# The norm ahead of the last feed-forward block: four of eight squares summed on TensorE, the sums and the spread one product sooner, the last output projection in order

## The chip, the cores and the metric

The kernel runs on one core of one Trainium2 chip. The metric is the time of one execution in microseconds on the device, lower is better. The engines are TensorE (PE in the profile, with its weight loads as PEld), VectorE (DVE), ScalarE (ACT), GpSimd (POOL) and SyncE (SP, which issues most transfers).

## The reference

One step of a streaming encoder of two layers over 640 frames (512 of a prompt, 8 times 16 of running streams) with 1024 features, in 32-bit floats. The part that matters here is the end of the attention layer and the feed-forward block behind it:

```python
def rms_norm(x, g):
    xf = x.astype(jnp.float32)
    y = xf * lax.rsqrt(jnp.mean(xf * xf, axis=-1, keepdims=True) + EPS)
    return (y * g.astype(jnp.float32)).astype(x.dtype)

def swiglu_ffn(h, g, w_in, w_out):
    a, b = jnp.split(rms_norm(h, g) @ w_in, 2, axis=-1)
    return h + (jax.nn.silu(a) * b) @ w_out
...
            h = h + o @ w_o[j]
        h = swiglu_ffn(h, norm_ffn[l], w_ffn_in[l], w_ffn_out[l])
    return rms_norm(h, norm_final), jnp.stack(new_hist, axis=0), k, v
```

`o` is the attention's output (16 heads of 64 features). The block's norm needs, for each frame, the mean of the squares of all 1024 features of `h`, and `h` is complete only when the whole output projection is added to it.

## The kernel before

`h` lies as 8 slices (`KT`) of 128 features by 640 frames, features on the partitions. Frames are worked in two halves of 320 (`NH`). A product in 32-bit precision is three matmuls with operands split in a high and a low part (`whi`, `wlo` for weights, `ohi`, `olo` for the attention's output).

The output projection adds the contributions of the head pairs in four rounds of two pairs. Rounds 0 to 2 are pieces of a stream of fill work (`set_o`, matmuls on L1272, additions to `h` on L1361) which runs between the steps of the attention. Round 3 is `halves(3, (mmt, amt), adds)`, the generator `fin`: first the 8 slices of the first half of the frames, then the 8 of the second half, each product six matmuls (L202, L203, L204) and one addition to `h` on VectorE (L1548), whose instruction is kept in `adds`. Its PSUM tiles come in turn from two pools of two buffers each: `mm` (`mmt`) for even slices and `am` (`amt`) for odd ones. The last steps of the attention use the same pools: two small transpositions (L1526) go to `mm` tiles, from which ScalarE makes `ohi` and VectorE `olo` (L190, L192), two small pieces each.

A scheduler orders the instructions of each engine by priority and by its own estimate of when they are ready; each engine then runs its list strictly in that order. `tc.issue_after(x)` keeps what is inside it behind `x`; `tc.high_priority` moves it ahead. `step_end[0]` is the last matmul of a step of the attention or of its fill work, `half_end[0]` the last matmul of the latest product of `fin`.

The norm of the first half of the frames is made while `fin` works on the second half:

- ScalarE squares the 8 slices of `h` as they are complete (`square`, L211) into `sqs`, and VectorE adds the eight squares to one (`acc`, L1616);
- after `MEAN_AT` products of the second half, three matmuls with the column `onec` of 1/1024 (one for each 128 frames, L1623) sum `acc` over the features, with the frames on the partitions; VectorE adds the epsilon (L1625) and POOL takes the power -0.5 (L1627);
- after `SPREAD_AT` products, three matmuls with the identity spread the result over all partitions (L257), and ScalarE copies it to `bw` (L1633);
- the feed-forward block begins with `bw`: VectorE normalises the slices (L601), ScalarE and VectorE split them into `XH` and `XL` (L374, L375), and TensorE starts with two accumulators of four (L442) in PSUM pools that take over the place of `mm` and `am`.

Ahead of that, the block's first weights are split in six pieces by ScalarE and VectorE (L374, L375: `shi`/`slo`, `hid`, `whi`/`wlo`); the list `lead` names the instruction behind which each piece stands.

Of the kernel before, what the change touches and what calls it, by code (L numbers as in the profile page):

```python
# [12 lines left out]
ALU = mybir.AluOpType  # L13
PSUM = bass.MemoryType.PSUM

P = 128
D = 1024
KT = D // P
# [15 lines left out]
EPS = 1e-6  # L34
NEG = -1e30

MEAN_AT, SPREAD_AT, STATS1_AT = 4, 6, 1
GR = ((0, 256), (256, 384))
GS = ((0, 320), (320, 320))

# [19 lines left out]
NH = NT // 2  # L60
# [25 lines left out]
def tile_trunk(ctx, tc, xT, vecs, hist, w_pw1, w_pw2, w_in0, w_out0, w_os0, w_in1, w_out1, w_os1,  # L86
               w_kq, w_v, w_o, rel, kc, vc, y_out, convp_out, convs_out, k_out, v_out):
    nc = tc.nc
# [8 lines left out]
    split_end = [None]  # L97
# [6 lines left out]
    def nm(s):  # L104
        uid[0] += 1
        return f"{s}_{uid[0]}"

    def mmt(n=512):
        return mm.tile([P, n], F32, tag="mm", name=nm("mm"))

    def w2t():
        return w2.tile([P, 1024], F32, tag="w2", name=nm("w2"))
# [17 lines left out]
    onec = cst.tile([P, 1], F32, name="onec", tag="onec")  # L130
# [76 lines left out]
    def square(s, n, eng="a", q=None):  # L207
        if q is None:
            q = tp.tile([P, tw[0]], F32, tag=sqt[0], name=nm("sq"))
        if eng == "a":  # L210
            norm_end["sq"] = nc.scalar.activation(out=q[:, :n], in_=s, func=AF.Square).ins  # L211
        else:
            e = nc.vector if eng == "v" else nc.gpsimd
            e.tensor_tensor(out=q[:, :n], in0=s, in1=s, op=ALU.mult)
        return q[:, :n]

    def tiles(n):
        return [min(t, n - P) for t in range(0, n, P)]
# [36 lines left out]
    def spread(st, r, n, ins=False):  # L255
        for t, a in enumerate(tiles(n)):
            end = nc.tensor.matmul(st[:, a:a + P], r[:, t:t + 1].to_broadcast([P, P]), ident,  # L257
                                   start=True, stop=True)
        norm_spread[0] = end.ins
        return end.ins if ins else st[:, :n]  # L260
# [945 lines left out]
    fill, step_end, spare_w2 = None, [None], [None, []]  # L1206
# [331 lines left out]
    def halves(r, tiles, adds):  # L1538
        wh, wl = wsplit(w_o[r], 16, P)
        for g0 in (0, NH):  # L1540
            for m in range(KT):
                pt = tiles[m % len(tiles)]()
                half_end[0] = mm3(
                    pt[:, :NH], [(wh[:, (k * 8 + m) * P:(k * 8 + m + 1) * P],
                                  wl[:, (k * 8 + m) * P:(k * 8 + m + 1) * P]) for k in range(2)],
                    [(oT[2 * r + k][0][:, g0:g0 + NH], oT[2 * r + k][1][:, g0:g0 + NH])
                     for k in range(2)]).ins
                adds.append(nc.vector.tensor_tensor(out=h[:, m, g0:g0 + NH], in0=pt[:, :NH],  # L1548
                                                    in1=h[:, m, g0:g0 + NH], op=ALU.add).ins)
                yield  # L1550
# [8 lines left out]
    for p in range(NP):  # L1559
# [8 lines left out]
        for op in BO[p].split():  # L1568
# [11 lines left out]
            i = int(op[1]) if len(op) > 1 else None  # L1580
# [25 lines left out]
    adds = []  # L1606
    fin = halves(3, (mmt, amt), adds)
    for _ in range(KT):
        next(fin)
    with tc.high_priority(offset=HP):  # L1610
        sqs = xp.tile([P, KT, 384], F32, tag="xl1", name=nm("sqs")).rearrange("p a n -> p (a n)")
        acc, r = sqs[:, KT * NH:(KT + 1) * NH], sqs[:, (KT + 1) * NH:(KT + 1) * NH + 8]
        for k in range(KT):
            sq = square(h[:, k, 0:NH], NH, "a", sqs[:, k * NH:(k + 1) * NH])
            if k:
                sq_end = nc.vector.tensor_tensor(out=acc, in0=acc if k > 1 else sqs[:, 0:NH],  # L1616
                                                 in1=sq, op=ALU.add).ins
    for _ in range(MEAN_AT):
        next(fin)
    with tc.issue_after(half_end[0]), tc.high_priority(offset=HP):  # L1620
        st, nt = w2t(), len(tiles(NH))
        for t, c in enumerate(tiles(NH)):
            end = nc.tensor.matmul(st[:, 512 + t:513 + t], acc[:, c:c + P], onec, start=True,  # L1623
                                   stop=True)
        eps_end = nc.vector.tensor_scalar(out=r[:, 0:nt], in0=st[:, 512:512 + nt], scalar1=EPS,  # L1625
                                          scalar2=None, op0=ALU.add).ins
        nc.gpsimd.tensor_tensor(out=r[:, 4:4 + nt], in0=r[:, 0:nt], in1=mhalf[:, :nt], op=ALU.pow)  # L1627
    for i in range(MEAN_AT, SPREAD_AT):
# [2 lines left out]
    with tc.issue_after(half_end[0]), tc.high_priority(offset=HP):  # L1631
        end = spread(st, r[:, 4:8], NH, True)
        nc.scalar.activation(out=bw, in_=st[:, :NH], func=AF.Copy)  # L1633
    for i in range(SPREAD_AT, KT):
        with tc.issue_after(end):
# [4 lines left out]

    hf = ExitStack()
    spare, products = ffn(1, w_in1, w_out1, w_os1, ((256, 384), (0, 256)), hf,
                                     [(split_end[0], i) for i in (adds[1], adds[3], adds[5], sq_end)] +
                                     [(eps_end,)] * 2,
                                     b0=bw)

# [70 lines left out]
    acc, bsb, bcs, sq, rs = {}, {}, {}, {}, {}  # L1717
# [16 lines left out]
    with tc.high_priority(offset=HP):  # L1734
        squares(0)
        st = mmt()
# [98 lines left out]
```

## Time and profile before

| | us |
|---|---|
| median of 3 runs (lowest to highest) | 1445.59 (1443.12 to 1446.67) |
| the profiled execution, its time | 1445.22 |
| the profiled execution, its span | 1443.4 |
| granted TensorE clock, mean | 0.998 |
| TensorE busy | 1420.6 (98%) |
| VectorE busy | 1118.9 (78%) |
| ScalarE busy | 748.6 (52%) |
| POOL busy | 284.3 (20%) |

The span runs from the first to the last instruction; the time is that of the whole execution. The stage of the change lies from 984 to 1007 us of the span. A row of the timeline gives the start, the length, the engine, the line, the operation, the tile that is written and those that are read, the shape, and the count of merged instructions; in brackets stands the idle time of the engine just before it and what ended it. Matmuls overlap, so their lengths are longer than the distance from one start to the next. A 32-bit matmul that is not split appears as two records (passes) in the profile, so that three of them are six.

### The profile page before, as it was taken

The page shows a single profiled execution, that of the slowest core. Times are in us where ns is not written, and L with a number is a line of the kernel's source. Part 1 is how long each engine was busy: PE and PEld are TensorE (multiplying, and loading weights), DVE is VectorE, ACT ScalarE, POOL GpSimd, SP SyncE. Part 2 cuts the span into 40 slices and gives each one's busy share as a digit, 9 for nine tenths or more (in the row PEclk, how much of TensorE's full clock was granted, in tenths as well). Part 3 has the DMA queues.
Part 4 walks back from the last instruction along what each step waited for, and adds up shares of the span by engine and source line. Part 5 has one row for each costly group of instructions (what it writes and reads, how often), then busy time and mean ns, then how long its engine had stood idle before and what let it go on. Part 6 is the DMA issues. An engine that isn't in the chain of part 4 may idle for free. (4 is left out here: it accounts for less than half of the span.)

```text
span 1443.4 us, 28243 instructions
## 1 busy us (share of the span) xinstructions
PE 1420.6 (98%) x11086; PEld 1366.8 (95%) x11086; DVE 1118.9 (78%) x2490; ACT 748.6 (52%) x1633; POOL 284.3 (20%) x335
## 2 busy tenths in 40 slices
PE   9999999999999999999999999999999999999998
PEld 8998799999999999999998898988999999999998
DVE  6789867899788788766666756667899788888755
ACT  5666554564554554445654454543654564554443
POOL 5689221011111111013111111110011111111101
PEclk9999999999999999999999999999999999999999
DMA  7267524054435444524555555562034544444522
GB/s 246 70 174 190 137 76 135 24 141 134 138 103 143 133 110 122 146 91 162 174 183 195 191 176 166 183 220 67 30 98 134 157 111 123 132 116 124 148 60 74
DMA packets 66934, 192.58 MB, mean 133 GB/s; under 512 B 12145, under 2 KB 30321, under 8 KB 58481
## 3 DMA queue, kind: packets, MB, share of 16 engines
q1 hardware_dynamic: 52432, 160.58, 34.2%
q0 software_dynamic: 13504, 29.37, 10.3%
q8 instruction: 87, 1.43, 0.4%
q10 hardware_dynamic: 864, 0.83, 0.2%
q14 instruction: 47, 0.38, 0.1%
HBM read 179.14 MB, written 11.61 MB: 132 GB/s over the span
## 5 line engine op out<-in xcount | busy, mean ns | idle before, releaser
L442 PE MATMUL mm<-XH,whi 128*128 128x320 f32 x896 | 275.9, 310 | 2.6 <-ACT t L454 2.6
L442 PE MATMUL mm<-XH,wlo 128*128 128x320 f32 x896 | 276.3, 309 | 0.0
L442 PE MATMUL mm<-XL,whi 128*128 128x320 f32 x896 | 274.6, 309 | 0.0
L374 ACT ACTIVATE whi<-raw 128x512 fp32r<-128x512 f32 (+2 forms) x280 | 168.7, 613 | 139.4 <-PE mm L442 109.6
L375 DVE TENSOR_TENSOR wlo<-raw,whi 128x512 fp32r<-128x512 f32 (+2 forms) x280 | 184.6, 667 | 22.3 <-ACT whi L374 21.0
L442 PE MATMUL mm<-hid,whi 128*128 128x320 f32 x732 | 172.0, 310 | 3.7 <-DVE hid L375 2.7
L442 PEld LDWEIGHTS mm<-XH,whi 128*128 128x128 f32 x896 | 167.8, 188 | 4.2 <-ACT t L454 4.2
L442 PEld LDWEIGHTS mm<-XH,wlo 128*128 128x128 f32 x896 | 168.2, 188 | 0.0
L442 PEld LDWEIGHTS mm<-XL,whi 128*128 128x128 f32 x896 | 167.7, 188 | 0.0
L442 PEld LDWEIGHTS mm<-hid,whi 128*128 128x128 f32 x732 | 124.9, 188 | 6.4 <-DVE hid L375 3.7
L202 PE MATMUL mm<-xh,whi 128*128 128x320 f32 (+2 forms) x416 | 129.3, 313 | 1.0 <-ACT xh L190 0.6
L203 PE MATMUL mm<-xh,wlo 128*128 128x320 f32 (+2 forms) x416 | 128.0, 310 | 0.0
L204 PE MATMUL mm<-xl,whi 128*128 128x320 f32 (+2 forms) x416 | 126.0, 310 | 0.0
L442 PE MATMUL mm<-hid,wlo 128*128 128x320 f32 x366 | 113.0, 309 | 0.0
L442 PE MATMUL mm<-XH,shi 128*128 128x320 f32 x344 | 106.0, 309 | 0.7 <-DVE h L1548 0.7
L442 PE MATMUL mm<-XH,slo 128*128 128x320 f32 x344 | 106.0, 308 | 0.0
L442 PE MATMUL mm<-XL,shi 128*128 128x320 f32 x344 | 105.5, 308 | 0.0
L420 POOL DMA_DIRECT2D s<-in_w_in x38 | 22.1, 582 | 375.8 <-DVE wlo L375 152.8
L844 POOL TENSOR_TENSOR ca<-ca,cvt 128x512 f32<-128x512 f32 x60 | 91.8, 1531 | 17.4 <-ACT cvt L841 10.9
L374 ACT ACTIVATE shi<-raw 128x512 fp32r<-128x512 f32 (+1 forms) x114 | 66.7, 588 | 45.1 <-PE mm L442 39.6
L454 ACT ACTIVATE t<-mm 128x320 f32<-128x320 f32 x114 | 49.5, 434 | 66.8 <-PE mm L442 66.5
L583 DVE TENSOR_TENSOR h<-h,mm 128x320 f32<-128x320 f32 x168 | 79.9, 481 | 5.3 <-PE mm L442 5.1
(337 smaller groups left out, 3696.7 us busy)
## 6 DMA issues: line engine op xcount, KB each, us to landing
raw<-in_w_in SPq DMA_DIRECT2D x38, 1024.0 KB
s<-in_w_in POOLq DMA_DIRECT2D x76, 256.0 KB, 4.2
raw<-in_w_os SPq DMA_DIRECT2D x24, 768.0 KB
cache<-in_ck SPq DMA_DIRECT2D x32, 512.0 KB
cache<-in_cv SPq DMA_DIRECT2D x32, 512.0 KB
raw<-in_w_pw SPq DMA_DIRECT2D x11, 1024.0 KB
s<-in_w_os POOLq DMA_DIRECT2D x48, 192.0 KB, 3.6
raw<-in_w_kq SPq DMA_DIRECT2D x8, 1024.0 KB
```

Of the source, the lines that this page charges most:

```text
L202: nc.tensor.matmul(ps, wh, xh, start=(first and i == 0), stop=False)
L203: nc.tensor.matmul(ps, wl, xh, start=False, stop=False)
L204: end = nc.tensor.matmul(ps, wh, xl, start=False, stop=(stop and i == last))
L374: put_end[1] = nc.scalar.activation(out=hi, in_=src, func=AF.Copy).ins
L375: put_end[0] = nc.vector.tensor_tensor(out=lo, in0=src, in1=hi.bitcast(F32), op=sub).ins
L420: nc.gpsimd.dma_start(s1, src[:, 2 * n:3 * n])
L442: last = nc.tensor.matmul(pt, wt, v, start=(first and k == i == 0), stop=(k == n - 1 and i == 2), skip_group_check=True)
L454: keeps.append(nc.scalar.activation(out=t, in_=pt, func=AF.Copy).ins)
L583: nc.vector.tensor_tensor(out=hv, in0=hv, in1=pt, op=sub if row else add)
L844: nc.gpsimd.tensor_tensor(out=acc, in0=acc, in1=pr, op=ALU.add)
```

## The change

It does four things.

- Of the eight squares only the first four are added on VectorE (`DIRECT = 4`). The sum of these and each of the four others go through the column `onec` on TensorE: 15 matmuls instead of 3. A reduction on VectorE adds the five partial sums of each frame ahead of the epsilon.
- The sums stand after 3 instead of 4 products of the second half, and the spread after 5 instead of 6.
- Each of the first eight products of `fin` stands behind the last step of the attention and its fill work (`tc.issue_after(step_end[0])`).
- The fourth piece of the block's weights stands behind `adds[7]`, the addition of the first half's last slice, and no longer behind the last addition of the squares.

```diff
-MEAN_AT, SPREAD_AT, STATS1_AT = 4, 6, 1
+MEAN_AT, SPREAD_AT, STATS1_AT, DIRECT = 3, 5, 1, 4
...
     for _ in range(KT):
-        next(fin)
+        with tc.issue_after(step_end[0]):
+            next(fin)
...
         for k in range(KT):
             sq = square(h[:, k, 0:NH], NH, "a", sqs[:, k * NH:(k + 1) * NH])
-            if k:
+            if 0 < k < DIRECT:
                 sq_end = nc.vector.tensor_tensor(out=acc, in0=acc if k > 1 else sqs[:, 0:NH],
                                                  in1=sq, op=ALU.add).ins
...
         st, nt = w2t(), len(tiles(NH))
-        for t, c in enumerate(tiles(NH)):
-            end = nc.tensor.matmul(st[:, 512 + t:513 + t], acc[:, c:c + P], onec, start=True,
-                                   stop=True)
-        eps_end = nc.vector.tensor_scalar(out=r[:, 0:nt], in0=st[:, 512:512 + nt], scalar1=EPS,
+        srcs = [acc] + [sqs[:, k * NH:(k + 1) * NH] for k in range(DIRECT, KT)]
+        w = len(srcs)
+        for i, s in enumerate(srcs):
+            for t, c in enumerate(tiles(NH)):
+                end = nc.tensor.matmul(st[:, 512 + t * w + i:513 + t * w + i], s[:, c:c + P], onec,
+                                       start=True, stop=True)
+        nc.vector.tensor_reduce(out=r[:, 0:nt], in_=st[:, 512:512 + nt * w].rearrange(
+            "p (t k) -> p t k", k=w), op=ALU.add, axis=mybir.AxisListType.X)
+        eps_end = nc.vector.tensor_scalar(out=r[:, 0:nt], in0=r[:, 0:nt], scalar1=EPS,
                                           scalar2=None, op0=ALU.add).ins
...
-                                     [(split_end[0], i) for i in (adds[1], adds[3], adds[5], sq_end)] +
+                                     [(split_end[0], i) for i in (adds[1], adds[3], adds[5], adds[7])] +
```

On TensorE, where the attention ends (the two transpositions on L1526) and the first products begin, the order before is this. `am_` and `mm_` are PSUM tiles of the two pools, with a number each:

```order
L1526 MATMUL mm_11838<-ident,Sn 128x128
L1526 MATMUL mm_11844<-ident,Ss_11635 128x128
L202 MATMUL am_11880<-ohi_11035,whi_11867 128x320
L203 MATMUL am_11880<-ohi_11035,wlo_11868 128x320
L204 MATMUL am_11880<-olo_11036,whi_11867 128x320
L202 MATMUL am_11896<-ohi_11035,whi_11867 128x320
L203 MATMUL am_11896<-ohi_11035,wlo_11868 128x320
L204 MATMUL am_11896<-olo_11036,whi_11867 128x320
L202 MATMUL am_11880<-ohi_11507,whi_11867 128x320
L203 MATMUL am_11880<-ohi_11507,wlo_11868 128x320
L202 MATMUL am_11896<-ohi_11507,whi_11867 128x320
L203 MATMUL am_11896<-ohi_11507,wlo_11868 128x320
```

Ten matmuls of two products of round 3 stand ahead of the stream's last two products, mm_11850 and mm_11858; their last two matmuls stand behind these. At the same place after the change:

```order
L1526 MATMUL mm_11838<-ident,Sn 128x128
L1526 MATMUL mm_11844<-ident,Ss_11635 128x128
L1272 MATMUL mm_11850<-ohi_9995,whi_11263 128x320
L1272 MATMUL mm_11850<-ohi_9995,wlo_11264 128x320
L1272 MATMUL mm_11850<-olo_9996,whi_11263 128x320
L1272 MATMUL mm_11850<-ohi_10543,whi_11263 128x320
L1272 MATMUL mm_11850<-ohi_10543,wlo_11264 128x320
L1272 MATMUL mm_11850<-olo_10544,whi_11263 128x320
L1272 MATMUL mm_11858<-ohi_9995,whi_11263 128x320
```

The stream's last two products now follow the transpositions at once, and am_11880, am_11896 and all the others come behind them, six matmuls each in one piece.

On TensorE around the sums, before (`w_1407` is the tile of the sums):

```order
L203 MATMUL mm_11968<-ohi_11507,wlo_11868 128x320
L204 MATMUL mm_11968<-olo_11508,whi_11867 128x320
L1623 MATMUL w_1407_11984<-onec,sqs_11936 128x1 x3
L202 MATMUL mm_11990<-ohi_11035,whi_11867 128x320
L203 MATMUL mm_11990<-ohi_11035,wlo_11868 128x320
```

And after:

```order
L203 MATMUL mm_11964<-ohi_11507,wlo_11868 128x320
L204 MATMUL mm_11964<-olo_11508,whi_11867 128x320
L1627 MATMUL w_1406_11972<-onec,sqs_11936 128x1 x15
L202 MATMUL am_11991<-ohi_11035,whi_11867 128x320
L203 MATMUL am_11991<-ohi_11035,wlo_11868 128x320
```

Fourteen products stand between the transpositions and the sums before, thirteen after (the stream's two, the eight of the first half, and four or three of the second half). Two products stand between the sums and the spread in both; behind the spread there are two before and three after.

On VectorE, from the epsilon to the split of the first normalised slices, before:

```order
L1625 TENSOR_SCALAR sqs_11936<-w_1407_11984 128x3
L375 TENSOR_TENSOR wlo_12066<-raw_12182,whi_12065 128x1024 x2
L1548 TENSOR_TENSOR h<-mm_11990,h 128x320
L1548 TENSOR_TENSOR h<-am_11998,h 128x320
L601 SCALAR_TENSOR_TENSOR hid_12076<-h,vec,bw 128x320 x2
L601 SCALAR_TENSOR_TENSOR hid_12077<-h,vec,bw 128x320 x2
L1548 TENSOR_TENSOR h<-mm_12010,h 128x320
L1548 TENSOR_TENSOR h<-am_12018,h 128x320
L375 TENSOR_TENSOR XL_1423_12047<-hid_12076,XH_1422_12046 128x320 x2
```

And after:

```order
L1629 TENSOR_REDUCE sqs_11936<-w_1406_11972 128x3
L1631 TENSOR_SCALAR sqs_11936<-sqs_11936 128x3
L375 TENSOR_TENSOR wlo_12075<-raw_12191,whi_12074 128x1024 x2
L1548 TENSOR_TENSOR h<-am_11991,h 128x320
L1548 TENSOR_TENSOR h<-mm_11999,h 128x320
L601 SCALAR_TENSOR_TENSOR hid_12085<-h,vec,bw 128x320 x2
L601 SCALAR_TENSOR_TENSOR hid_12086<-h,vec,bw 128x320 x2
L1548 TENSOR_TENSOR h<-am_12011,h 128x320
L1548 TENSOR_TENSOR h<-mm_12019,h 128x320
L1548 TENSOR_TENSOR h<-am_12027,h 128x320
L375 TENSOR_TENSOR XL_1423_12056<-hid_12085,XH_1422_12055 128x320 x2
```

The reduction is new, and three additions to `h` instead of two stand behind the normalisation, with that of the mm tile second. ScalarE, POOL and SyncE keep their order.

## The prediction

> **What bounds the kernel now.** I read the page first, then the busy time by stretch behind the change, then the waits of the weight loads around it, then the order in time there, engine by engine.
>
> ```profile
> span 1443.4 us, 28243 instructions
> ...
> PE 1420.6 (98%) x11086; PEld 1366.8 (95%) x11086; DVE 1118.9 (78%) x2490; ACT 748.6 (52%) x1633; POOL 284.3 (20%) x335
> ```
>
> TensorE is busy 98% of the span, so a change is worth what it does to TensorE's waits and to TensorE's own work; a VectorE addition taken away is worth nothing by itself. The next question is whether a shift at the change can be lost again afterwards:
>
> ```profile
> 1006.40:1020.40 14.00, 14.00 (x96) 14.00 (x97) 11.91 (x24) 9.28 (x18) 0.00 (x0) 1.00 0.26 101
> ...
> 1022.30:1049.50 27.20, 27.20 (x189) 27.20 (x189) 24.44 (x66) 14.98 (x34) 0.00 (x0) 1.00 0.00 1
> 1049.50:1100.00 50.50, 47.91 (x319) 46.42 (x318) 46.30 (x100) 29.76 (x66) 7.23 (x10) 1.00 0.48 126
> ```
>
> The columns are the stretch, its length, then PE, weight loads, VectorE, ScalarE, POOL. From 1006.40 to 1049.50 the weight loads leave no hole, and from 1049.50 to 1100.00 TensorE lacks 50.50 - 47.91 = 2.59 us in all. So nearly all of a shift at 1006 reaches the end. 96 matmuls in 14.00 us are 0.146 us each: a product of the output projection (six matmuls of 320 columns) is 0.88 us.
>
> Around the change (984 to 1007 us) the weight loads wait five times:
>
> ```profile
> PEld w L1623 <- DVE sqs L1616: 1.8, 1, 1.8
> PEld mm L442 <- DVE h L1548: 0.9, 1, 0.9
> PEld am L202 <- ACT ohi L190: 0.8, 1, 0.8
> PEld w L257 <- POOL sqs L1627: 0.5, 1, 0.5
> PEld mm L442 <- ACT XH L374: 0.2, 1, 0.2
> ```
>
> In sum 4.2 us: more the change cannot gain here. In time, on TensorE:
>
> ```profile
> 984.66 0.39 PE L202 MATMUL am<-ohi,whi 128*128 128x320 f32 x1
> ...
> 986.33 0.41 PE L202 MATMUL am<-ohi,whi 128*128 128x320 f32 x1 [0.53 <-ACT ohi L190]
> ...
> 997.72 0.31 PE L204 MATMUL mm<-olo,whi 128*128 128x320 f32 x1
> 999.54 0.83 PE L1623 MATMUL w<-onec,sqs 128*128 128x1 f32 x6 [1.51 <-DVE sqs L1616]
> 1000.23 0.39 PE L202 MATMUL mm<-ohi,whi 128*128 128x320 f32 x1
> ...
> 1001.92 0.31 PE L204 MATMUL am<-olo,whi 128*128 128x320 f32 x1
> 1002.50 0.93 PE L257 MATMUL w<-ident,sqs 128*128 128x128 f32 x6 [0.27 <-POOL sqs L1627]
> 1003.19 0.40 PE L202 MATMUL mm<-ohi,whi 128*128 128x320 f32 x1
> ...
> 1005.12 0.42 PE L442 MATMUL mm<-XH,shi 128*128 128x320 f32 x1
> 1005.37 0.31 PE L442 MATMUL mm<-XH,slo 128*128 128x320 f32 x1
> 1006.34 0.41 PE L442 MATMUL mm<-XH,shi 128*128 128x320 f32 x1 [0.67 <-DVE h L1548]
> ```
>
> And on the engines that release it:
>
> ```profile
> 986.18 0.23 DVE L192 TENSOR_TENSOR olo<-mm,ohi 64x64 fp32r<-64x64 f32 x1 [0.15 <-ACT ohi L190]
> ...
> 986.18 0.37 DVE L192 TENSOR_TENSOR olo<-mm,ohi 64x64 fp32r<-64x64 f32 x2 [0.15 <-ACT ohi L190]
> ...
> 995.30 0.47 ACT L211 ACTIVATE sqs<-h 128x320 f32<-128x320 f32 x1 [0.33 <-DVE h L1548]
> ...
> 1000.41 0.16 DVE L1625 TENSOR_SCALAR sqs<-w 128x3 f32<-128x3 f32 x1 [0.32 <-PE w L1623]
> ...
> 1000.49 2.35 DVE L375 TENSOR_TENSOR wlo<-raw,whi 128x1024 fp32r<-128x1024 f32 x2
> ...
> 1000.72 1.73 POOL L1627 TENSOR_TENSOR sqs<-sqs,mhalf 128x3 f32<-128x3 f32 x1 [28.30 <-DVE sqs L1625]
> ...
> 1003.47 0.44 ACT L1633 ACTIVATE bw<-w 128x320 f32<-128x320 f32 x1 [7.70 <-PE w L257]
> ...
> 1003.94 1.94 DVE L601 SCALAR_TENSOR_TENSOR hid<-h,vec,bw 128x320 f32<-128x320 f32 x4 [0.31 <-ACT bw L1633]
> ...
> 1005.80 0.49 DVE L1548 TENSOR_TENSOR h<-mm,h 128x320 f32<-128x320 f32 x1
> 1006.20 0.48 DVE L1548 TENSOR_TENSOR h<-am,h 128x320 f32<-128x320 f32 x1
> ```
>
> The chain to read: sums, epsilon, power on POOL, spread, copy to bw, four norms (L601), and behind them in VectorE's fixed order the last additions to h, of which the one on an mm tile frees the PSUM buffer of the block's second accumulator at 1006.34. I take that matmul as the end of the stage.
>
> **The change, part by part.**
>
> 1. The eight first products stand in order behind the previous projection's last two (mm_11850, mm_11858). Before, TensorE ran six am matmuls while it waited; now mm_11850 is the very next instruction. Its pool has two buffers, and its own still holds mm_11838, the first small transposition. Its last reader is the third of VectorE's four small subtractions, 986.18 + 0.23 = 986.41. With the 0.05 us that stand between such an end and TensorE's next start in the rows above (the addition's 1005.80 + 0.49 to 1006.34), mm_11850 starts at 986.46 instead of 984.66: a wait of 1.80 us where there was one of 0.8 (ohi is ready by then). Cost 1.00. Behind it all eight products are queued. Bounds: no wait at all if the buffer came free earlier (-0.8), or the fourth subtraction, 986.18 + 0.37 = 986.55 (+1.1). I take +1.0, since the third is the reader in program order.
>
> 2. Thirteen products, not fourteen, stand ahead of the sums: -0.88. TensorE is there at 997.87 + 1.00 - 0.88 = 997.99. Four additions (L1616) are gone; the last square's product is the tenth of thirteen, done three products earlier, at 995.35. Addition 0.48, square 0.47 (row at 995.30) and one queued addition of 0.40 make 996.7, so 1.3 us of cover. The wait of 1.5 goes, and the sums start at 997.99 instead of 999.54.
>
> 3. Fifteen matmuls of one column instead of three, two passes each: 30 for 6. The next block's norm has the same kind, 18 passes:
>
> ```profile
> 1020.38 0.72 PE L243 MATMUL w<-onec,acc 128*128 128x1 f32 x6
> 1020.97 1.48 PE L243 MATMUL w<-onec,hid 128*128 128x1 f32 x12
> 1022.30 0.39 PE L442 MATMUL mm<-XH,wlo 128*128 128x320 f32 x1
> ...
> 1022.48 0.17 DVE L247 TENSOR_REDUCE rst<-w 128x3 f32<-128x9 f32 x1 [0.46 <-PE w L243]
> 1022.68 0.17 DVE L280 TENSOR_SCALAR rst<-rst 128x3 f32<-128x3 f32 x1
> ```
>
> 1.92 us for 18 is 0.107 us a pass; 0.69 for six (999.54 to 1000.23) is 0.115. 24 more passes cost 2.56 to 2.76; I take 0.107, from the longer run. They are pure TensorE work: nothing hides them. The last pass starts at 997.99 + 29 x 0.107 = 1001.09, against 999.54 + 5 x 0.115 = 1000.1 before.
>
> 4. The reduction ahead of the epsilon: 0.20 us from its start to the next one's (1022.48 to 1022.68), on the chain. VectorE waits for the sums with the two weight subtractions (2.35 us, row at 1000.49) behind it, which end near 1004.1, and two additions to h, to 1004.9; the norms start at about 1005.1, so 0.2 of cover. The weight load that these subtractions release moves by 1.2 us, less than its readers.
>
> 5. The spread follows the last pass by 1002.50 - 1000.1 = 2.4, now 2.6: 1003.69, so 1.19 later than before. TensorE is through its two products at about 1003.1 and waits 0.6 (0.4 before).
>
> 6. Three products instead of two behind the spread, hence three additions behind the norms: am, mm, am. The one that frees the buffer is now second, 0.40 later (1005.80 to 1006.20). Before, 3.84 us lay from the spread's start to 1006.34; now 4.24: the stage ends at 1003.69 + 4.24 = 1007.93. TensorE itself is ready at 1003.69 + 0.69 + 3 x 0.88 + 0.1 + 0.3 = 1007.4, so this wait stays (0.5).
>
> 7. The fourth weight piece hangs on adds[7] and not on the last sum: VectorE does it earlier, in the cover of step 2, at no cost.
>
> The sum: 1007.93 - 1006.34 = +1.6 us. As TensorE's account: wait +1.0, passes +2.56, power +0.2, against the sums' wait -1.6, the end's -0.3, and -0.2 of refilling after waits, which here shows as a first spacing of 0.25 (1005.12 to 1005.37). The change takes out a 1.5 us wait and pays with 2.56 us of work on the engine that is 98% busy. The profiled execution took 1445.22 us (span 1443.4), 0.37 under the median of the runs, 1445.59; +1.6 on the median gives 1447.2. With the bounds (start wait -0.8 to +1.1, passes to 2.76) the stage gives -0.2 to +1.9.
>
> **The rivals.**
>
> Clock (slower). In one place of this trace a norm cost TensorE its clock:
>
> ```profile
> 27.05 0.77 PE L243 MATMUL w<-onec,w 128*128 128x1 f32 x6
> ...
> 25.81:29.22 3.41, 2.21 (x17) 2.09 (x16) 1.04 (x4) 1.36 (x3) 2.17 (x4) 1.00 0.58 77
> 29.23:32.63 3.40, 3.40 (x17) 3.40 (x17) 2.09 (x5) 1.51 (x4) 1.62 (x1) 0.50 0.81 325
> ...
> 1019.09:1022.50 3.41, 3.41 (x29) 3.41 (x29) 1.69 (x4) 0.49 (x2) 0.00 (x0) 1.00 0.00 0
> ```
>
> Six one-column passes and a wait of 1.2 us were followed by 3.4 us at a granted clock of 0.50. The 30 passes now take 3.2 us in one piece. If such passes count as idle, the same can follow here: 3.4 us at half speed lose up to 1.7, so +3.3 and 1448.9; from a second such stretch on it is +5.0 (1450.6) and over the bound. Against it: 18 passes in 1.9 us (last row, with 1.5 us of full matmuls) left the clock at 1.00. The Trainium skill says in "TensorE: Matmul & The Clock Gate", section "What's actually happening", that the array falls to half clock after at least one idle window of about 3.4 us, and that these windows run freely. The length agrees with the 3.4 us at 0.50 here, but a window with TensorE busy 2.21 of 3.41 us was enough, so the trace asks for less than a whole idle window. By that rule taken strictly, 3.2 us of passes would be too short and the sum stays +1.6; by the row it may be +3.3.
>
> Buffer free (not slower). If mm_11850 needn't wait, its 1.8 us go: 1.6 - 1.8 = -0.2, 1445.4. For it: before, this product ran later and met no wait, so no row shows when its buffer came free. Against it: a pool of two, with the two transpositions just ahead.
>
> Absorbed later. Of the 2.59 us that TensorE lacks from 1049.50 on, some may be waits for loads that do not shift: at best all of the 1.6, 1445.6. Against it: VectorE's chain shifts by the same 1.6, as its additions stand at the stage's end.
>
> A true gain of over 0.3% (4.3 us) would need all 4.2 us of waits and free passes; nothing speaks for it.
>
> **How the numbers follow.** Forecast (+0.8 to +2.2) 0.58; clock once 0.17; buffer free 0.10; absorbed 0.07; slower beyond the bound by a second clock stretch 0.06; faster beyond it 0.02. A measurement of this kernel tells about 0.3%, 4.3 us, from no change. Of clock-once I count 0.04 as over it, since the three runs shown lie 3.5 us apart: slower 0.10, faster 0.02, same 0.88. The range takes in 1445.4 and 1448.9 and about 1.2 us of the runs' own spread on both ends: 1444.2 to 1450.2.
>
> **What would show it.** Right: TensorE idle for about 1.8 us ahead of the first L1272 matmul on an mm tile, released by VectorE's olo; no wait ahead of the sums; 30 passes in 3.2 us; a wait of 0.5 to 0.6 for POOL; the wait for h L1548 at the block's start kept at about 0.5; the second accumulator 1.6 us later against the start of the stage. Wrong: no wait at the first L1272 matmul (step 1), a wait at the sums (step 2), another price of a pass (step 3), or a granted clock under 1.00 between 998 and 1010 us.

## The result, and the profile after

| | before | after |
|---|---|---|
| median of 21 runs each, us (lowest to highest) | 1445.49 (1442.77 to 1447.35) | 1448.06 (1446.31 to 1452.26) |
| after / before, 95% interval | | 1.0020 (1.0015 to 1.0026) |
| profiled execution, time and span, us | 1445.22, 1443.4 | 1447.31, 1445.5 |
| granted clock, mean over the profiled execution | 0.998 | 0.997 |

The change costs 2.2 to 3.8 us by the interval, 2.57 by the medians. That is less than the 4.3 us taken as the bound beforehand, but no doubt is left about its sign. The forecast was +1.6 us, at full clock.

The page's first lines of the kernel after (span; busy time, share and count of each engine):

```profile
span 1445.5 us, 28286 instructions
...
PE 1423.4 (98%) x11110; PEld 1370.2 (95%) x11110; DVE 1117.8 (77%) x2487; ACT 749.6 (52%) x1633; POOL 281.1 (19%) x335
```

TensorE has 24 records more (the passes) and 2.8 us more busy time; VectorE has three instructions fewer (four additions gone, one reduction new) and 1.1 us less. The work went from an engine with room to the one without.

The waits of the weight loads around the change in the kernel after (984 to 1009 us; tile and line, releaser: sum in us, count, longest), all that are listed there:

```profile
PEld mm L1272 <- issue: 1.9, 1, 1.9
PEld mm L442 <- DVE h L1548: 0.6, 1, 0.6
```

The waits for `sqs` ahead of the sums and for POOL ahead of the spread, 1.8 and 0.5 us before, are gone. A wait of 1.9 us ahead of the first product of the stream stands in place of the 0.8 us for `ohi`. The timeline of the kernel after on TensorE, and the releasers on VectorE, ScalarE and POOL:

```profile
984.08 0.27 PE L1526 MATMUL mm<-ident,Ss 128*128 128x128 f32 x1
...
986.01 0.38 PE L1272 MATMUL mm<-ohi,whi 128*128 128x320 f32 x1 [1.66 <-DVE olo L192]
...
997.37 0.31 PE L204 MATMUL mm<-olo,whi 128*128 128x320 f32 x1
997.52 3.40 PE L1627 MATMUL w<-onec,sqs 128*128 128x1 f32 x30
1000.78 0.39 PE L202 MATMUL am<-ohi,whi 128*128 128x320 f32 x1
...
1003.60 0.47 PE L204 MATMUL mm<-olo,whi 128*128 128x320 f32 x1
1003.87 1.14 PE L257 MATMUL w<-ident,sqs 128*128 128x128 f32 x6
...
1007.48 0.31 PE L442 MATMUL mm<-XH,shi 128*128 128x320 f32 x1
...
1008.31 0.42 PE L442 MATMUL mm<-XH,shi 128*128 128x320 f32 x1 [0.37 <-DVE h L1548]
```

```profile
996.16 0.47 ACT L211 ACTIVATE sqs<-h 128x320 f32<-128x320 f32 x1 [0.32 <-DVE h L1548]
...
1000.96 0.17 DVE L1629 TENSOR_REDUCE sqs<-w 128x3 f32<-128x15 f32 x1 [2.75 <-PE w L1627]
1001.16 0.17 DVE L1631 TENSOR_SCALAR sqs<-sqs 128x3 f32<-128x3 f32 x1
...
1001.51 1.70 POOL L1633 TENSOR_TENSOR sqs<-sqs,mhalf 128x3 f32<-128x3 f32 x1 [29.62 <-DVE sqs L1631]
```

To read: the first product stands 1.93 us behind the start of the last transposition (986.01 - 984.08), released by the small subtractions of `olo`; the last of the first half's squares is done at 996.16 + 0.47 = 996.63, ahead of the sums at 997.52, which start without a wait; 30 passes; the reduction 0.20 us ahead of the epsilon; the h-wait at the second accumulator at the end. Each was foretold. What was not in the forecast but in its rival shows in the lengths: the last matmul ahead of the spread takes 0.47 us where the one ahead of the sums takes 0.31, and the six passes of the spread 1.14 where they took 0.93 before. The busy time by stretch in the kernel after (stretch, length, busy time and count of PE, PEld, DVE, ACT, POOL, then the granted clock, the DMA share and GB/s):

```profile
997.68:1001.08 3.40, 3.40 (x31) 3.40 (x32) 0.61 (x2) 0.00 (x0) 0.00 (x0) 1.00 0.55 219
1001.09:1004.49 3.40, 3.40 (x15) 3.40 (x14) 3.25 (x6) 0.00 (x0) 1.70 (x1) 0.50 0.00 0
1004.51:1007.91 3.40, 3.40 (x24) 3.16 (x23) 2.48 (x7) 2.19 (x5) 0.00 (x0) 1.00 0.93 308
```

Right behind the passes TensorE ran 3.41 us at half clock. It shows as no wait at all: PE is busy 3.40 of 3.40 us in all three stretches.

To compare executions I use distances from the start of the last transposition (L1526 on `Ss`) to the first matmul of the block's second accumulator (the third L442), called the stage, and from there to the start of the last instruction, called the rest. In the kernel before, the stage runs from this row to the start at 1006.34 in the prediction's rows:

```profile
984.63 0.27 PE L1526 MATMUL mm<-ident,Ss 128*128 128x128 f32 x1
```

In the table the first three columns count from that transposition too:

| us | first product | sums, first to last pass | spread | stage | rest |
|---|---|---|---|---|---|
| before | 0.03 | 14.91 to 15.49 | 17.87 | 21.71 | 436.99 |
| forecast for after, full clock | 1.83 | 13.36 to 16.46 | 19.06 | 23.30 | |
| after | 1.93 | 13.44 to 16.59 | 19.79 | 24.23 | 437.18 |

The stage is 24.23 - 21.71 = 2.52 us longer and the rest 0.19. Ahead of the stage, where the change does nothing, the profile after is 0.55 us shorter (984.63 to 984.08), so that the two spans differ by 2.16; over the ten profiles of this study that part ends between 982.26 and 984.63. The difference of the medians (2.57) is about that of the stage. Up to the last pass the forecast is hit within 0.13 us, and from there on it is late by 0.7 to 0.9 us. The question for the experiments was whether that is the half clock, and whether the half clock belongs to the change or to chance.

### The profile page after: what moved, and what is told of

Read it like the earlier page. It is cut to its first block, busy times and chain, and to the rows that moved or that the text cites. A ratio compares the mean times of both kernels' runs of the same rounds, so it can differ in the third digit from the quotient of the medians.

```text
span 1445.5 us, 28286 instructions
## 1 busy us (share of the span) xinstructions
PE 1423.4 (98%) x11110; PEld 1370.2 (95%) x11110; DVE 1117.8 (77%) x2487; ACT 749.6 (52%) x1633; POOL 281.1 (19%) x335
## 4 chain that ended last, share of the span: by engine, by line
PE 89%; DVE 6%; DMA 3%; ACT 1%; issue 1%; POOL 0%; DVEq 0%; POOLq 0%; ACTq 0%
PE mm L442 47%; PE mm L1272 10%; PE mm L202 6%; PE mm L204 6%; PE mm L203 6%; PE mm L888 3%; PE w L1272 2%; DMA raw<-in_w_os 1%; DMA raw<-in_w_in 1%; PE am L1445 1%; PE am L1517 1%; PE am L1461 1%; DVE wlo L375 1%; PE w L1416 1%; PE w L1479 1%; PE mm L149 1%
## 5 line engine op out<-in xcount | busy, mean ns | idle before, releaser
L442 PE MATMUL mm<-XH,whi 128*128 128x320 f32 x896 | 275.8, 310 | 3.2 <-ACT t L454 2.6
L442 PE MATMUL mm<-XH,wlo 128*128 128x320 f32 x896 | 276.1, 309 | 0.0
L442 PE MATMUL mm<-XL,whi 128*128 128x320 f32 x896 | 274.5, 309 | 0.0
L442 PE MATMUL mm<-hid,whi 128*128 128x320 f32 x732 | 172.0, 310 | 3.8 <-DVE hid L375 2.2
L442 PEld LDWEIGHTS mm<-XH,whi 128*128 128x128 f32 x896 | 167.8, 188 | 5.0 <-ACT t L454 4.2
L442 PEld LDWEIGHTS mm<-XH,wlo 128*128 128x128 f32 x896 | 168.2, 188 | 0.0
L442 PEld LDWEIGHTS mm<-XL,whi 128*128 128x128 f32 x896 | 167.7, 188 | 0.0
L442 PEld LDWEIGHTS mm<-hid,whi 128*128 128x128 f32 x732 | 124.9, 188 | 6.6 <-DVE hid L375 3.2
L442 PE MATMUL mm<-hid,wlo 128*128 128x320 f32 x366 | 113.0, 309 | 0.0
L442 PE MATMUL mm<-XH,shi 128*128 128x320 f32 x344 | 105.8, 309 | 0.4 <-DVE h L1548 0.4
L442 PE MATMUL mm<-XH,slo 128*128 128x320 f32 x344 | 106.0, 308 | 0.0
L442 PE MATMUL mm<-XL,shi 128*128 128x320 f32 x344 | 105.5, 308 | 0.0
```

The costliest lines, as they stand in the source:

```text
L442: last = nc.tensor.matmul(pt, wt, v, start=(first and k == i == 0), stop=(k == n - 1 and i == 2), skip_group_check=True)
```

## The experiments

Theory: +1.6 to +1.7 us of work and waits, and on top of it the clock that the 30 passes in one block cost. Rivals: the half clock comes and goes by itself and has nothing to do with the passes; the wait at the first product is what costs; the edges of the sums and the spread (three and five products) are what costs.

**The first products not in order.** The changed kernel without its third part:

```diff
-        with tc.issue_after(step_end[0]):
-            next(fin)
+        next(fin)
```

> The changed kernel with the order of the first eight products undone; the 15 sums, 3 and 5 products and the tie to adds[7] stay. Measure: the stage from the start of the second small transposition (L1526 on Ss) to the first matmul of the second accumulator (third L442), 21.71 us before and 24.23 us in the changed kernel, which had 3.4 us of half clock in it. My account (start wait 1.0, 24 passes 2.56, sums' wait -1.6, small terms, and 0.9 for the half clock where it falls): the wait at the start goes from 1.8 back to 0.8, the sums still don't wait, the stage is 22.3 us at full clock and 23.2 with a half-clock stretch; time 0.6 to 1.5 us over the kernel before. Rival, that the order costs nothing because later waits swallow it: 23.3 at full clock, 24.2 with the stretch.

Measured: median 1446.12 us of 11 runs against 1444.02 of before, ratio 1.0016 (1.0007 to 1.0025). The first product stands 0.03 us behind the transposition again, and the sums start at 12.37 us of the stage, 1.07 sooner than in the kernel after: up to the sums, the wait of step 1 costs what it was put at (+1.0). But the stage took 24.64 us, longer than with the order and outside what was expected (22.3, or 23.2 with one stretch at half clock). The ends of the stage, the sums, and the stretches of this kernel:

```profile
982.26 0.27 PE L1526 MATMUL mm<-ident,Ss 128*128 128x128 f32 x1
...
994.63 4.28 PE L1626 MATMUL w<-onec,sqs 128*128 128x1 f32 x30
...
1006.90 0.41 PE L442 MATMUL mm<-XH,shi 128*128 128x320 f32 x1 [0.24 <-DVE h L1548]
...
993.53:996.93 3.40, 3.40 (x31) 3.40 (x29) 1.66 (x4) 0.47 (x1) 0.00 (x0) 1.00 0.82 286
996.95:1000.34 3.39, 3.39 (x16) 3.39 (x16) 1.36 (x3) 0.00 (x0) 0.84 (x1) 0.50 0.03 11
1000.36:1003.75 3.39, 3.39 (x16) 3.39 (x15) 2.12 (x4) 0.12 (x1) 0.83 (x1) 0.50 0.35 70
```

Half clock again, here over two stretches, and the first of them falls into the passes: 22 passes took 2.43 us at full clock, the other eight 1.71 at half, 0.21 us each. By these rows the clock took back all that the missing wait had gained: between the sums and the spread lie 7.49 us here (12.37 to 19.86), 6.35 in the kernel after. The profiled execution (1447.33 us) is the third slowest of the eleven. What the order costs the changed kernel's stage at full clock stays open, since no profile shows the block of 30 at full clock.

**The order alone.** The kernel before with the third part of the change only:

```diff
-        next(fin)
+        with tc.issue_after(step_end[0]):
+            next(fin)
```

> The kernel before with only the order of the first eight products. If the terms simply add: start wait 1.8, the stage 22.7 us, time +1.0. If VectorE's chain of additions, and not TensorE, sets when the sums can start, the later arrival of TensorE is swallowed by the 1.6 us wait at the sums: stage 21.7 to 22.2, time 0 to +0.5. I expect the second. No half clock in either.

Measured: median 1443.37 us against 1444.02, ratio 0.9998 (0.9989 to 1.0006). The waits of the weight loads in its stage:

```profile
PEld mm L1272 <- issue: 1.9, 1, 1.9
PEld mm L442 <- DVE h L1548: 0.9, 1, 0.9
PEld w L257 <- POOL sqs L1628: 0.5, 1, 0.5
PEld w L1624 <- DVE sqs L1617: 0.4, 1, 0.4
```

The wait of 1.9 us at the first product is there, yet the sums start at 14.59 us, 0.32 sooner than before, and the stage is 21.38 us, 0.33 shorter. The wait at the sums, 1.8 us in the kernel before, is 0.4 here. With all eight squares added on VectorE, it is VectorE's chain that sets when the sums may start (the last row), and a wait of TensorE ahead of them is paid out of the wait at the sums. That part of the expectation held; the stage is still shorter than the 21.7 to 22.2 us expected, and why VectorE's chain was done 0.3 us sooner was not traced. No stretch of this stage was at half clock. So the order is no loss by itself; the sums come later for it only where they have nothing else to wait for, as in the kernel after.

**The same passes, not in one block.** The changed kernel with the same 15 column matmuls, but in three groups of three and one of six, with a product or more between the groups; VectorE adds the four later squares, so that the four first can go through the column early:

```diff
-            if 0 < k < DIRECT:
+            if k > DIRECT:
...
+    for i, k in enumerate((1, 3, 0, 2)):
+        with tc.issue_after(half_end[0]), tc.high_priority(offset=HP):
+            end = one_sum(i, sqs[:, k * NH:(k + 1) * NH])
+        if i < MEAN_AT:
+            with tc.issue_after(end.ins):
+                next(fin)
+    with tc.issue_after(end.ins), tc.high_priority(offset=HP):
+        end = one_sum(DIRECT, acc)
```

> The changed kernel with the same 30 passes, but squares 0 to 3 go to TensorE directly, one by one between products, and squares 4 to 7 are added on VectorE, so that no stretch of passes is longer than about 1.3 us. If the long stretch of one-column passes brings the half clock: granted clock 1.00 in the whole stage, stage 23.3 us, time +1.6 over before. If the half clock comes from elsewhere it shows up here as well, and stage 24.2. If TensorE's 24 more passes cost nothing by themselves: stage 21.7.

Measured: median 1444.77 us against 1444.02, ratio 1.0007 (0.9999 to 1.0016). The ends of the stage, the passes and the start of the spread in the timeline, one of the waits of the weight loads, and the whole stage as one stretch:

```profile
984.00 0.27 PE L1526 MATMUL mm<-ident,Ss 128*128 128x128 f32 x1
...
993.05 0.72 PE L1624 MATMUL w<-onec,sqs 128*128 128x1 f32 x6
...
996.37 0.72 PE L1624 MATMUL w<-onec,sqs 128*128 128x1 f32 x6
...
997.92 0.72 PE L1624 MATMUL w<-onec,sqs 128*128 128x1 f32 x6
...
999.46 1.39 PE L1624 MATMUL w<-onec,sqs 128*128 128x1 f32 x12
...
1003.20 0.38 PE L257 MATMUL w<-ident,sqs 128*128 128x128 f32 x1 [0.48 <-POOL sqs L1641]
...
1007.43 0.41 PE L442 MATMUL mm<-XH,shi 128*128 128x320 f32 x1 [0.37 <-DVE h L1548]
...
PEld w L257 <- POOL sqs L1641: 0.7, 1, 0.7
...
984.00:1007.40 23.40, 20.92 (x149) 20.19 (x147) 17.73 (x39) 10.79 (x23) 1.69 (x1) 1.00 0.25 86
```

All 30 passes are there, the clock is 1.00 throughout, and the last pass starts at 16.60 us, where it does in the kernel after (16.59). From there on the order on TensorE, VectorE and ScalarE is the same in both, and the clock differs: spread at 19.19 us (19.79 after), stage 23.43 us (24.23). This is the forecast's sum met at full clock, 23.30 foretold, with 4.24 us from the spread to the second accumulator as worked out. The half clock cost the kernel after 24.23 - 23.43 = 0.80 us, by one profile of each. The medians against before (+0.75 here, +2.57 after, each against its own runs of before) lie further apart than that.

**All eight squares direct.** More of the same cause: 48 passes in one block.

```diff
-MEAN_AT, SPREAD_AT, STATS1_AT, DIRECT = 3, 5, 1, 4
+MEAN_AT, SPREAD_AT, STATS1_AT, DIRECT = 3, 5, 1, 1
...
-        srcs = [acc] + [sqs[:, k * NH:(k + 1) * NH] for k in range(DIRECT, KT)]
+        srcs = [sqs[:, 0:NH]] + [sqs[:, k * NH:(k + 1) * NH] for k in range(DIRECT, KT)]
```

> The changed kernel with all eight squares summed on TensorE, 48 passes in one piece (5.1 us) and no addition of squares on VectorE. Passes at 0.107 us: 1.9 us more than in the changed kernel; a half clock is granted behind the stretch in every execution if such passes count as idle, since 5.1 us is longer than the 3.4 us of a stretch: stage 26.1 to 27.0 us, time 4.4 to 5.3 over before. If the passes don't count as idle: clock 1.00, stage 25.2, time +3.5. If passes cost nothing by themselves: no more than the changed kernel.

Measured: median 1450.16 us of 5 runs against 1444.02, ratio 1.0048 (1.0036 to 1.0061); the slowest of all. The stretches:

```profile
997.53:1000.93 3.40, 3.40 (x33) 3.40 (x32) 0.34 (x1) 0.00 (x0) 0.00 (x0) 1.00 0.34 133
1000.96:1004.35 3.39, 3.39 (x17) 3.39 (x17) 0.30 (x3) 0.00 (x0) 0.00 (x0) 0.50 0.00 0
1004.37:1007.76 3.39, 3.39 (x15) 3.39 (x14) 3.04 (x5) 0.00 (x0) 1.70 (x1) 0.50 0.08 10
```

A stretch of nothing but passes, then two at half clock. The stage is 27.86 us, 3.63 more than with 30 passes. At 0.107 us the 18 more passes are 1.93. Of the other 1.70, passes at half clock make 1.38: 13 of them took 2.77 us, 0.21 each. The last 0.3 was not traced. I had put the stage at 26.1 to 27.0: the price of a pass at half clock was missing.

**The changed kernel again, twice**, on another chip than the four above, to see whether the half clock comes back.

> The changed kernel, unchanged, profiled once more. If the half clock behind the 30 passes falls by the phase of a free-running window, it may be missing here: then the stage is 23.3 us (24.23 with 3.4 us of half clock), with a wait of about 0.6 us for POOL ahead of the spread, and 24.6 or so with two windows of it. If it is fixed to this place in the program: 24.23 again.

> The changed kernel, unchanged, a further time: as for the one before. The point to which the half clock begins should again lie a whole number of 3.413 us steps from the other changes of the clock in the same execution.

Measured: 1446.48 and 1447.13 us, one run each, against a median of 1443.93 of before on that chip; stages of 24.24 and 24.13. Both have the stretch at half clock behind the passes; that of the first one and the one ahead of it, then the same of the second:

```profile
996.48:999.88 3.40, 3.40 (x33) 3.40 (x31) 0.75 (x2) 0.00 (x0) 0.00 (x0) 1.00 0.64 249
999.90:1003.29 3.39, 3.39 (x14) 3.39 (x15) 2.60 (x5) 0.00 (x0) 1.70 (x1) 0.50 0.00 0
```

```profile
998.31:1001.71 3.40, 3.40 (x30) 3.40 (x31) 0.67 (x3) 0.00 (x0) 0.15 (x1) 1.00 0.37 151
1001.73:1005.12 3.39, 3.39 (x16) 3.33 (x15) 2.71 (x4) 0.12 (x1) 1.52 (x1) 0.50 0.28 36
```

**The sums and the spread not sooner.** The changed kernel with the old places:

```diff
-MEAN_AT, SPREAD_AT, STATS1_AT, DIRECT = 3, 5, 1, 4
+MEAN_AT, SPREAD_AT, STATS1_AT, DIRECT = 4, 6, 1, 4
```

> The changed kernel with the sums and the spread at 4 and 6 products again. Fourteen products ahead of the sums: +0.88; two additions instead of three behind the norms: -0.4. Stage 23.8 us at full clock, 24.7 with one window of half clock. If one product sooner was worth nothing: 23.3 and 24.2.

Measured: 1446.37 us in one run, stage 25.13 us where 24.7 was expected, with the half clock from 999.43 to 1002.84. The sums stayed where they were (13.45 us): a product of the `mm` pool slipped behind them, so that thirteen products stand ahead as in the kernel after, and three between the sums and the spread. The spread came at 21.00 us, 0.89 later than in the first of the two repeats, just one product. So of "one product sooner", the spread's place is worth 0.9 us of the stage (25.13 against 24.24, one profile each, both with one stretch at half clock), and it is a gain that the change kept; the sums' place could not be tried on its own.

**The order and the spread later.** The order alone left VectorE's chain ahead of the second accumulator as the longest wait (0.9 us above); one product more ahead of the spread moves that accumulator's addition forward. The kernel before with the order and:

```diff
-MEAN_AT, SPREAD_AT, STATS1_AT = 4, 6, 1
+MEAN_AT, SPREAD_AT, STATS1_AT = 4, 7, 1
```

> A version that might beat both: the kernel before with the order of the first eight products (which gave a stage of 21.38 us) and the spread after seven products instead of six, the sums as before after four. Three products (2.7 us) then cover POOL's power (2.4 us), so the wait for POOL goes (-0.4), the spread comes 0.4 later, and only one addition, on an am tile, stands behind the norms, so that the second accumulator no longer waits for an addition (-0.8 to -1.0): stage 20.8 to 21.0 us, time 0.6 to 0.9 under the kernel before. If the start of the block is set by the copy to bw and the norms instead: stage 21.4 to 21.8 and no gain.

Measured: median 1443.60 us of 11 runs against 1443.93, ratio 0.9990 (0.9981 to 0.9999). The waits in its stage, and the second accumulator's first matmul, whose start at 1003.91 needs no wait of its own:

```profile
PEld mm L1272 <- issue: 1.9, 1, 1.9
PEld mm L442 <- ACT XH L374: 1.1, 1, 1.1
PEld w L1624 <- DVE sqs L1617: 0.4, 1, 0.4
PEld mm L442 <- DVE h L1548: 0.3, 1, 0.3
...
1003.51 0.42 PE L442 MATMUL mm<-XH,shi 128*128 128x320 f32 x1 [0.80 <-ACT XH L374]
1003.76 0.31 PE L442 MATMUL mm<-XH,slo 128*128 128x320 f32 x1
1003.91 0.31 PE L442 MATMUL mm<-XH,shi 128*128 128x320 f32 x1
```

The stage is 20.91 us, 0.80 shorter than before: the wait for `h` has shrunk, and one for the split of the normalised slices (`XH`) of 1.1 us has taken its place. It is the shortest stage of all. The whole execution is 0.1 to 2.7 us shorter than before, at the edge of what can be told, and that interval overlaps the one of the order alone.

The stages and the whole executions side by side; the second column is the stage minus that of before (21.71), the third what the ratio's interval makes of 1445 us:

| kernel | stage, difference | whole, difference | half clock in the stage |
|---|---|---|---|
| after | +2.52 | +2.2 to +3.8 | yes |
| first products not in order | +2.93 | +1.0 to +3.6 | yes, twice |
| order alone | -0.33 | -1.6 to +0.9 | no |
| passes spread out | +1.72 | -0.1 to +2.3 | no |
| all eight direct | +6.15 | +5.2 to +8.8 | yes, twice |
| order, spread later | -0.80 | -2.7 to -0.1 | no |

Each stage of one profile agrees with the interval of its runs. The clock parts them too, in the mean over all runs of a kernel. With a block of 30 or more passes it is 0.9967 over the 21 runs of the kernel after, 0.9971 over the 11 with the first products not in order, and 0.9952 over the five with 48 passes. Without a block it is 0.9980 and 0.9982 over the 27 and 15 runs of before on the two chips of the experiments, 0.9986 over the 11 with the order alone, and 0.9988 with the passes spread out and with the order and the spread later. One stretch at half clock takes 3.41 x 0.5 / 1445 = 0.0012 off the mean, so the kernel after has about one more of them than before, and the one with 48 passes about two. By its mean, the one with the first products not in order has fewer than the two that its profile shows.

## Why the prediction was right, and where not

The forecast of 1447.2 us lies 0.9 us under the median after, on a change of 2.57; sign and place were right, and one rival that was given 0.17 happened.

- **Step 1, the wait at the first product (+1.0): right.** 1.93 us from the transposition to the product against 1.83 foretold, released by the subtractions of `olo`. The rival "buffer free" is refuted by that row. Without the order the sums came 1.07 us sooner. Not foretold was that this wait is no loss with the sums as they were before: alone it left the stage 0.33 us shorter.
- **Step 2, no wait at the sums: right.** 13.44 us against 13.36.
- **Step 3, the price of a pass (0.107): right at full clock.** First to last pass 3.15 us against 3.10. At half clock a pass costs 0.21, which the sum did not have.
- **Step 4, the reduction (0.20): right,** 1000.96 to 1001.16.
- **Step 5, the spread 2.6 us behind the last pass: right at full clock** (16.60 to 19.19 with the passes spread out, 2.59), not in the kernel after (3.20). The wait for POOL of 0.6 us is there with the passes spread out (0.7) and gone in the kernel after, where TensorE itself was late: its two products ran at half clock.
- **Step 6, 4.24 us from the spread to the second accumulator: right** with the passes spread out; 4.44 in the kernel after, part of whose spread ran at half clock. The wait for `h` stayed (0.6 against 0.5).
- **Step 7, the fourth weight piece at no cost:** no row speaks against it, but it was not tried by itself.
- **The step that failed is the weight given to the clock.** I held 18 passes without an effect against six passes and a wait with one, and gave a single stretch at half clock a chance of 0.17. The two rows do not contradict each other: from the first pass to the next full product or spread they are 1.92 us (1020.38 to 1022.30) and 1.97 us (27.05 to 29.02), and 3.2 us lies far beyond both. All three profiles of the changed kernel had the stretch at half clock. The profiles of its three variants with 30 or more passes in one block had it too; in those with six passes, or with 30 spread out, the stage was at full clock. The sum should have been +1.6 and a clock's share.
- **The rival's price was too high.** It said 1.7 us at most and took 1.7. Measured were 0.8: until the spread the stretch cost 0.60 (19.79 against 19.19), since the slow products used up the wait for POOL, and behind the spread 0.20, since there VectorE's chain decides and not TensorE. +1.72 of work and waits (stage with the passes spread out against before) and 0.80 of clock are the 2.52 of the stage.
- **"Absorbed later" is refuted:** the rest is 436.99 us before and 437.18, 436.89 and 437.05 in three executions after. To take back 1.6 us it would have had to be 435.4; no profile of this study is under 436.2.

## What to carry to other kernels

Before work is moved from an engine with room to the one that is busy 98% of the time, set the wait that it removes (1.5 us here) against the work it adds (2.6 us): the wait has a ceiling, the work has none. A wait is not a cost by itself: the same 1.9 us wait was free while a wait behind it was longer, and put the sums 1.07 us later once that one was gone. Small matmuls that belong together are better dealt out between full products than issued as a block: the same 30 took 0.8 us less of the stage here.

## What the runs showed of the hardware

**A block of one-column passes brings the half clock, as idle time does.** PE and its weight loads were recorded as busy for the whole 3.40 us of the stretch with the passes, and the next 3.41 us were granted half the clock. The count of passes by stretch, over the profiles of this study (a stretch is 3.41 us on a grid of the execution's own, taken from where its clock changed; the time is that of the passes alone, each up to the next start):

| stretch | passes, time in them | other matmuls | clock of the next stretch |
|---|---|---|---|
| before, 1019.09 | 18, 1.92 us | 9 | 1.00 |
| passes spread out, 996.92 | 15, 1.50 us | 12 | 1.00 |
| after, second repeat, 998.31 | 22, 2.46 us | 6 | 0.50 |
| first products not in order, 993.53 | 22, 2.43 us | 7 | 0.50 |
| after, 997.68 | 27, 3.01 us | 2 | 0.50 |
| after, first repeat, 996.48 | 28, 3.12 us | 3 | 0.50 |
| sums and spread not sooner, 996.01 | 29, 3.23 us | 2 | 0.50 |
| first products not in order, 996.94, itself at 0.50 | 8, 1.71 us | 6 | 0.50 |
| after, first repeat, 999.88, itself at 0.50 | 2, 0.43 us | 11 | 1.00 |

In stretches at full clock the point lies between 1.9 and 2.4 us of such passes. In those already at half clock 1.7 us beside six other matmuls were enough to stay there, and no passes or two beside eleven were not. That the passes count by the share of the array that they use was not tried; only their number and place were.

The profiles show this point more sharply at a norm near 27 us of the span, which no run changed: six passes, then TensorE idle for 1.2 us until the spread. In six of the ten profiles the next stretch was at half clock (in the kernel before at 29.23), in the four others it was not. Passes and idle time together, as far as they fall into one stretch, took 1.97 to 1.99 us in the six. In the four they took 1.94 (first products not in order), 1.90 (order, spread later), 1.59 (order alone) and 1.47 us (after). The nearest of the four, in which the stretch took in all six passes and the whole wait, and the clock stayed at 1.00:

```profile
27.68 0.72 PE L243 MATMUL w<-onec,w 128*128 128x1 f32 x6
29.62 0.93 PE L257 MATMUL w<-ident,rst 128*128 128x128 f32 x6 [1.22 <-POOL rst L287]
...
27.55:30.95 3.40, 2.18 (x19) 2.09 (x19) 1.03 (x4) 1.36 (x3) 2.27 (x2) 1.00 0.48 97
30.97:34.37 3.40, 3.40 (x27) 3.40 (x26) 3.40 (x7) 1.85 (x4) 1.85 (x2) 1.00 0.67 270
```

If passes and idle time count alike, which no run tried apart, the point at full clock lies between 1.94 and 1.97 us, and the 18 passes of 1.92 us lie just under it.

The Trainium skill says in "TensorE: Matmul & The Clock Gate", section "What's actually happening", that the fall to half clock follows an idle window of about 3.4 us, and that these windows run freely. The length and the grid agree: every change of clock within an execution lies a multiple of 3.41 us from the others (in the kernel after 1001.09 and 1004.50), and where it lies against the program differs from one execution to the next (in the three of the changed kernel the half clock began 3.57, 2.96 and 4.15 us behind the first pass). "Idle" does not agree with the busy column: a stretch with 3.40 of 3.40 us busy counted. So the block of 30 passes, 3.2 us long, need not fill a window; where the grid cuts it near its middle, neither part has 1.97 us, and such an execution would escape. With a point at 1.95 us, a block of 3.26 us (997.52 to 1000.78) and a grid of 3.41, that is (2 x 1.95 - 3.26) / 3.41, about one execution in five, an estimate. None of the three profiles shows one, so how often it happens is not shown.

**At half clock a pass of one column costs twice as much**, 0.21 us against 0.107: so its time goes with the granted clock, as a fixed time of issue would not.
